# Hybrid DeltaNet and sparse attention decoder: the transposed inverse of the first doubling made by a transposition on VectorE

## The chip, the cores and the metric

The kernel runs on one core of one Trainium2 chip. The metric is the device time of one launch in microseconds (us). A core has five engines that run their own instruction queues and wait for each other by semaphores: TensorE (PE in the profile, with its weight loads as PEld), VectorE (DVE), ScalarE (ACT), GpSimd (POOL) and SyncE (SP, which issues most DMAs). TensorE's clock is granted by a throttle at one of two levels, 1.2 or 2.4 GHz; a granted clock of 1.00 is 2.4 GHz and 0.50 is 1.2 GHz.

## The reference

Two decoder layers over 528 tokens (16 meta tokens and 512). Each layer has a projection, two groups of heads side by side, an output projection, and a mixture of experts. The group that matters here is a gated DeltaNet with four heads of 128, which works in chunks and needs the inverse of a unit lower triangular matrix for every chunk and head:

```python
kb = k * beta[..., None]
lower = jnp.where(strict, jnp.einsum('bnhid,bnhjd->bnhij', kb, k) * decay, 0.0)
eye = jnp.eye(CHUNK, dtype=q.dtype)
tmat = lax.linalg.triangular_solve(eye + lower, jnp.broadcast_to(eye, lower.shape),
                                   left_side=True, lower=True, unit_diagonal=True)
u = tmat @ (v * beta[..., None])
w = tmat @ (kb * jnp.exp(gc)[..., None])
...
_, o = lax.scan(step, s0, xs)          # the recurrence over the chunks
```

Beside it, the other group of heads scores all earlier tokens with an indexer, keeps the 128 best keys of each query (`top_k`), and attends to them.

## The kernel before

**Tiling.** Tokens stand in five tiles: 16 meta tokens and four tiles of 128. The kernel uses chunks of 128 tokens where the reference has 64. Heads are handled in pairs, so one call of `invert` makes eight inverses of 128 by 128 (two heads by four tiles). There are two calls for each layer, `I0` and `I1` in the list `ORDER`, so four in a launch: they reach the changed lines at about 136 us (layer 0, pair 0), 283 us (layer 0, pair 1), 859 us (layer 1, pair 0) and 1011 us (layer 1, pair 1).

**The inversion.** `L4` is the strictly lower part, transposed. The 16 by 16 diagonal blocks are gathered through DRAM (`scr`, SP's lines 656 to 660), inverted by forward substitution on VectorE (lines 668 and 670), and brought back (`scx`, lines 673 to 680). `X` then holds the 16 by 16 inverses on the diagonal of 32 by 32 blocks, and line 683 makes `XT`, the same blocks transposed, with VectorE's transposition. Three doublings follow, from 16 to 32, 64 and 128. The first one (lines 684 to 702) makes `Y = -(L X)` masked, by 32 products of 32 by 32 (tile `y16`), then the off-diagonal blocks by products (tile `d16`), and adds them to `X` and to `XT`. Both are used below: `X` by the `y32` products and the copies to `X64`, `XT` by the copies to `F` (lines 712 and 714) and by the `d32` products. In the trace `X` and `XT` are both called `scores` (they lie in that unit's scratch), `Y` is `dn`, `F` is `lx`, and the PSUM tiles `y16` and `d16` are `y` and `d`.

**What sets the order.** The program is written in the order of `ORDER`, which mixes the work of the two groups of heads (`X` indexer, `H`, `P`, `I`, `R`, `E` DeltaNet, `S` selection, `Z`, `q`, `k`, `v` projections, `A` attention). A scheduler with its own model of durations then places the instructions of each engine, so an edit can move other instructions. Each engine runs its queue strictly in order. A product of two float32 operands through `_mm` stands as two matmuls in the trace. Projections (`project`, tile `pj`) are split into high and low parts, 24 matmuls for a half of 264 columns.

The list `ORDER`, and the helper that records all these products on line 61:

```python
ORDER = ("X0 H1 H0 P0 C0 I0 X1 H2 C1 X2 X3 C2 R0 Z0 C3 H3 q0 S1 Z1 q1 S2 P1 q2 S3 k0 q3 k1 Z3 k2 I1 k3 E0 Z2 v0 R1 v1 v2 v3 A0 S4 A1 A2 E1 A3 A4").split()
...
def _mm(nc, out, lhsT, rhs, start=True, stop=True):
    return nc.tensor.matmul(out, lhsT=lhsT, rhs=rhs, start=start, stop=stop)
```

Of the kernel before, what the change touches and what calls it, by code (L numbers as in the profile page):

```python
# [21 lines left out]
OP = mybir.AluOpType  # L22
# [37 lines left out]
def _mm(nc, out, lhsT, rhs, start=True, stop=True):  # L60
    return nc.tensor.matmul(out, lhsT=lhsT, rhs=rhs, start=start, stop=stop)  # L61
# [3 lines left out]
def trunk(ctx, tc, a, out, dbg=None, depth=DEPTH, stop=None):  # L65
    nc = tc.nc
# [207 lines left out]
    for l in range(depth):  # L274
# [93 lines left out]
        for t0, t1 in ((0, 4), (4, 5)):  # L368
            p = pc("smp")
# [50 lines left out]
        with tc.issue_after(soft.ins):  # L420
# [7 lines left out]
        p = pb("gcp")  # L428
# [10 lines left out]
                                op=OP.subtract)  # L439
# [207 lines left out]
        def invert(Hs, LT, full):  # L647
# [3 lines left out]
            X, XT = (scratch[:, 320 * i:320 * i + 320].rearrange("p (q c) -> p q c", q=10) for i in range(2))  # L651
# [15 lines left out]
            for i in range(1, 16):  # L667
                nc.vector.tensor_tensor(tv[:NB, :i, :i], Xv[:NB, :i, :i], Dv[:NB, i:i + 1, :i].to_broadcast([NB, i, i]),  # L668
                                        op=OP.mult)
# [16 lines left out]
            p = pc("y16")  # L686
            py = p[:, 0:256].rearrange("p (q c) -> p q c", q=8)
            for b in range(4):
                s = slice(32 * b, 32 * b + 32)
                for q in range(8):  # L690
                    _mm(nc, py[s, q, :], L4[s, q, s], X[s, q, :])
            Y = Db.rearrange("p (q c) -> p q c", q=8)
            nc.vector.tensor_tensor(Y, py, cst[:, None, C_M16:C_M16 + 32].to_broadcast([P, 8, 32]), op=OP.mult)
            p = pc("d16")
            pd = p.rearrange("p (x q c) -> p x q c", x=2, q=8)
            for b in range(4):
                s = slice(32 * b, 32 * b + 32)
                for q in range(8):
                    _mm(nc, pd[s, 0, q, :], XT[s, q, :], Y[s, q, :])
                    _mm(nc, pd[s, 1, q, :], Y[s, q, :], XT[s, q, :])  # L700
            nc.vector.tensor_tensor(X[:, :8, :], X[:, :8, :], pd[:, 0], op=OP.add)
            nc.vector.tensor_tensor(XT[:, :8, :], XT[:, :8, :], pd[:, 1], op=OP.add)

            F = full.rearrange("p (q i) -> p q i", q=8)
            nc.gpsimd.memset(full, 0.0)
# [3 lines left out]
            for b in range(4):  # L709
                s = slice(32 * b, 32 * b + 32)  # L710
# [6 lines left out]
            p = pc("y32")  # L717
            py = p[:, 0:256].rearrange("p (q c) -> p q c", q=8)
            Y = Db.rearrange("p (q c) -> p q c", q=8)
# [6 lines left out]
            p = pc("d32")  # L726
            pd = p.rearrange("p (x q c) -> p x q c", x=2, q=8)
# [9 lines left out]
            p = pc("y64")  # L737
            py = p.rearrange("p (q c) -> p q c", q=8)
            Y = XY
# [3 lines left out]
            p = pc("d64")  # L743
            pd = p.rearrange("p (q c) -> p q c", q=8)
# [115 lines left out]
        def delta_invert(pair):  # L860
            invert(*pairs[pair][:3])
# [155 lines left out]
        for j, src in ((0, zt), (1, so)):  # L1017
            for k in range(4):
                s = slice(k * T + q0, (k + 1) * T)
# [89 lines left out]
        for t in torder:  # L1109
            n, x = CNT[t], h[t][:CNT[t]]  # L1110
# [86 lines left out]
        for t, n in enumerate(cnts):  # L1197
            c = slice(t * 32, (t + 1) * 32)
# [32 lines left out]
        for c in range(2):  # L1231
            s = slice(64 * c, 64 * c + 64)
            nc.vector.scalar_tensor_tensor(gix[s], high[:, c, :], 8.0, low[:, c, :], op0=OP.mult, op1=OP.add)
        for c in range(2):
            s = slice(64 * c, 64 * c + 64)
# [515 lines left out]
```

## Time and profile before

| what | value |
|---|---|
| three timed runs | 1451.44, 1451.05, 1445.53 us (median 1451.05) |
| the profiled execution's own time | 1451.2 us |
| its span, first to last instruction | 1449.4 us |
| mean granted TensorE clock | 0.944 |
| TensorE busy | 1270.5 us, 88% of the span |
| VectorE, GpSimd, ScalarE busy | 788.2, 597.4, 544.1 us |

Busy shares are means over stages with different limits: in each layer, projections and the indexer come first, then selection beside the DeltaNet, then attention, then the experts. A group of rows names an engine, the line of the kernel, the operation, the tile written and the tiles read; "idle before" is the time for which the engine stood still ahead of the instruction, with what ended that. A line of stages gives, for each engine, busy time and (x) the number of its instructions in the stage, then the granted clock, the DMA engines' busy share and GB/s.

### The profile page before, as it was taken

What the parts mean: (1) busy time and instruction counts of PE and PEld (TensorE: products, weight loads), DVE (VectorE), ACT (ScalarE), POOL (GpSimd) and SP (SyncE); (2) the same over time, 40 slices, a digit from 0 to 9 for tenths busy, and PEclk for the clock granted to TensorE, in tenths of its full rate; (3) what the DMA queues carried; (4) which work ended last, traced back from release to release, by engine and by line L of the source; (5) the groups of instructions that cost most, each with busy time, mean ns of one, the idle gap of its engine ahead of it and who ended that gap; (6) DMA issues with size and microseconds to landing.
All of it is one profiled execution on the core that took longest, in us unless ns stands there. A gap on an engine that the chain in (4) does not pass through costs nothing.

```text
span 1449.4 us, 24501 instructions
## 1 busy us (share of the span) xinstructions
PE 1270.5 (88%) x8920; PEld 908.1 (63%) x8920; DVE 788.2 (54%) x2088; ACT 544.1 (38%) x1385; POOL 597.4 (41%) x779
## 2 busy tenths in 40 slices
PE   6999999899996998878588999998999789987883
PEld 6998999787883332223268988988887543322232
DVE  4887999667436141112568878995573431311116
ACT  3574544355322232223145745353453122222222
POOL 4556498845023111121255574897241231111102
PEclk9999999999997999999799999998699989999997
DMA  4252123224617999999722521222246389999991
GB/s 167 81 194 73 66 84 90 67 89 148 260 62 270 404 409 360 410 410 405 249 90 74 187 90 59 96 83 66 74 176 252 129 303 409 409 409 410 410 359 75
DMA packets 103694, 306.58 MB, mean 212 GB/s; under 512 B 24567, under 2 KB 25671, under 8 KB 103568
## 3 DMA queue, kind: packets, MB, share of 16 engines
q1 hardware_dynamic: 88464, 274.11, 49.9%
q0 software_dynamic: 9184, 18.00, 3.4%
q10 hardware_dynamic: 5920, 12.85, 2.4%
q8 instruction: 72, 1.18, 0.3%
q14 instruction: 54, 0.44, 0.1%
HBM read 281.49 MB, written 32.19 MB: 216 GB/s over the span
## 4 chain that ended last, share of the span: by engine, by line
PE 30%; DVE 7%; issue 5%; DMA 3%; ACT 3%; POOL 1%; SPq 1%; POOLq 0%; ACTq 0%; DVEq 0%; another core or an unknown queue 0%
PE pj L61 8%; PE h L61 7%; PE yp L61 4%; PE d L61 1%; PE po L987 1%; DMA ytab<-yw,dest 1%; PE lgp L61 1%; DVE dn L668 1%; PE ptp L979 1%; PE xtq L1373 1%; DVE dn L521 1%; PE y L61 1%; PE vp L61 1%; PE ix L61 1%; POOL wl L226 1%
## 5 line engine op out<-in xcount | busy, mean ns | idle before, releaser
L226 POOL TENSOR_TENSOR wl<-wr,wh 128x256 fp32r<-128x256 f32 (+1 forms) x296 | 250.3, 876 | 224.6 <-ACT wh L221 182.4
L61 PE MATMUL h<-we,xT 128*64 128x512 f32 x1024 | 229.9, 600 | 1.4 <-DMA we<-w 1.2
L61 PE MATMUL pj<-hh,wh 128*128 128x264 f32 (+2 forms) x928 | 165.3, 315 | 6.7 <-ACT raw L338 3.6
L61 PEld LDWEIGHTS h<-we,xT 128*64 128x64 f32 x1024 | 73.5, 140 | 145.5 <-issue 134.7
L61 PE MATMUL pj<-hl,wh 128*128 128x264 f32 (+2 forms) x928 | 161.8, 309 | 0.9 <-DVE rs L1624 0.9
L61 PE MATMUL pj<-hh,wl 128*128 128x264 f32 (+2 forms) x928 | 158.8, 305 | 0.0
L61 PE MATMUL yp<-we,hidT 128*64 128x512 f32 x512 | 133.2, 657 | 26.8 <-ACT yw L1355 23.1
L61 PEld LDWEIGHTS pj<-hh,wh 128*128 128x128 f32 (+1 forms) x928 | 135.1, 197 | 13.4 <-ACT raw L338 4.1
L61 PEld LDWEIGHTS pj<-hl,wh 128*128 128x128 f32 (+1 forms) x928 | 136.2, 195 | 6.8 <-DVE rs L1624 1.1
L1242 POOL MEMSET xe<- 128x1024 f32 x32 | 30.4, 952 | 263.8 <-PE h L61 249.3
L61 PEld LDWEIGHTS pj<-hh,wl 128*128 128x128 f32 (+1 forms) x928 | 131.9, 190 | 5.1 <-issue 0.4
L1325 DVE SCALAR_TENSOR_TENSOR hid<-hid,h 128x256 f32<-128x256 f32 x32 | 13.5, 421 | 212.4 <-ACT hid L1324 212.4
L221 ACT CAST wh<-wr 128x1024 fp32r<-128x1024 f32 (+1 forms) x82 | 85.5, 1046 | 92.3 <-PE pj L61 41.9
L1324 ACT ACTIVATE hid<-h 128x256 f32<-128x256 f32 x32 | 12.3, 384 | 227.3 <-PE h L61 215.9
L1380 ACT ACTIVATE xT<-xtq,lcol 128x128 f32<-128x128 f32 x192 | 73.6, 456 | 58.9 <-PE xtq L1373 58.3
L61 PEld LDWEIGHTS yp<-we,hidT 128*64 128x64 f32 x512 | 34.6, 144 | 91.7 <-issue 53.2
L1378 DVE TENSOR_SCALAR xT<-xtq,lcol 128x128 f32<-128x128 f32 x64 | 26.2, 410 | 119.3 <-ACT xT L1380 119.3
L521 DVE SCALAR_TENSOR_TENSOR dn<-cin,cw,dn 128x528 f32<-128x528 f32 x72 | 64.0, 897 | 10.8 <-ACT dn L519 9.7
L1492 POOL DMA_INDIRECT ytab<-yw,dest x28 | 28.2, 1008 | 88.4 <-ACT xT L1380 45.9
L496 DVE MATCH_REPLACE8 scores<-top,scores 128x144 f32<-128x144 f32 (+3 forms) x128 | 62.0, 487 | 0.0
L495 DVE MAX8 top<-scores 128x8 f32<-128x144 f32 (+3 forms) x128 | 60.5, 494 | 0.2
L1335 PE MATMUL hidT<-cst,hid 128*128 128x128 f32 x64 | 14.0, 300 | 39.7 <-DVE hid L1326 39.7
(432 smaller groups left out, 2488.2 us busy)
## 6 DMA issues: line engine op xcount, KB each, us to landing
we<-w SPq DMA_DIRECT2D x190, 1024.0 KB, 19.5
wr<-w_in SPq DMA_DIRECT2D x64, 512.0 KB, 3.5
wr<-w_out SPq DMA_DIRECT2D x16, 512.0 KB, 3.6
yr<-ytab SPq DMA_DIRECT2D x16, 512.0 KB, 11.8
ytab<-zr ACTq DMA_DIRECT2D x16, 264.0 KB, 3.2
hu<-x SPq DMA_DIRECT2D x8, 512.0 KB, 5.1
hs<-hu ACTq DMA_DIRECT2D x8, 512.0 KB, 4.8
ytab<-zr ACTq DMA_DIRECT2D x16, 256.0 KB, 3.2
```

What stands on the lines that cost most here:

```text
L61: return nc.tensor.matmul(out, lhsT=lhsT, rhs=rhs, start=start, stop=stop)
L221: nc.scalar.copy(hi[:, :KT * m], raw)
L226: eng.tensor_tensor(lo[:, c], raw[:, c], hi[:, c], op=OP.subtract)
L495: nc.vector.max(top, sc)
L496: nc.vector.match_replace(out=sc, in_to_replace=top, in_values=sc, imm_value=GONE)
L521: nc.vector.scalar_tensor_tensor(dst, cin[:, j:j + T], cw[:, ci + j:ci + j + 1], dst, op0=OP.mult, op1=OP.add)
L668: nc.vector.tensor_tensor(tv[:NB, :i, :i], Xv[:NB, :i, :i], Dv[:NB, i:i + 1, :i].to_broadcast([NB, i, i]), op=OP.mult)
L979: nc.tensor.transpose(p[:, (tk - 1) * P:tk * P], lg[:, OFF[tk]:OFF[tk] + P], ident)
L1242: nc.gpsimd.memset(xe, 0.0)
L1378: last = nc.vector.tensor_scalar(xT[:, kk, :], src, g_, b_, op0=OP.mult, op1=OP.add)
L1380: nc.scalar.activation(xT[:, kk, :], src, AF.Identity, bias=b_, scale=g_)
L1492: nc.gpsimd.indirect_dma_start(out=ytab[:, :], out_offset=bass.IndirectOffsetOnAxis(ap=dest[:, pair:pair + 1], axis=0), in_=yw[:, :], in_o ...
```

## The change

Before, the first doubling made two sets of products into one PSUM bank: `XT` by `Y` for `X` and `Y` by `XT` for `XT`, and VectorE added each set to its own matrix. After, only the first set is made, and `XT` is written by VectorE's 32 by 32 transposition of the updated `X`. The updated blocks are complete 32 by 32 blocks on the diagonal, so transposing each block gives the same matrix that the second set of products and its addition gave.

```diff
             p = pc("d16")
-            pd = p.rearrange("p (x q c) -> p x q c", x=2, q=8)
+            pd = p[:, 0:256].rearrange("p (q c) -> p q c", q=8)
             for b in range(4):
                 s = slice(32 * b, 32 * b + 32)
                 for q in range(8):
-                    _mm(nc, pd[s, 0, q, :], XT[s, q, :], Y[s, q, :])
-                    _mm(nc, pd[s, 1, q, :], Y[s, q, :], XT[s, q, :])
-            nc.vector.tensor_tensor(X[:, :8, :], X[:, :8, :], pd[:, 0], op=OP.add)
-            nc.vector.tensor_tensor(XT[:, :8, :], XT[:, :8, :], pd[:, 1], op=OP.add)
+                    _mm(nc, pd[s, q, :], XT[s, q, :], Y[s, q, :])
+            nc.vector.tensor_tensor(X[:, :8, :], X[:, :8, :], pd, op=OP.add)
+            nc.vector.transpose(XT[:, :8, :].rearrange("p q c -> p (q c)"), X[:, :8, :].rearrange("p q c -> p (q c)"))
```

Lines of the changed kernel behind this place have a number lower by one: the addition to `X` is line 700 there and the transposition line 701. The scheduler's order moves at some places too. Three are shown.

VectorE's queue at the first inversion (layer 0, pair 0), before: the two additions stand one behind the other (`d_1202` is the tile `d16`, `raw` a rotated projection, `lx` the matrix `F`).

```order
L348 TENSOR_TENSOR raw<-raw,ru 128x512
L483 SCALAR_TENSOR_TENSOR scores<-rel,wi,scores 128x144
L349 TENSOR_TENSOR raw<-raw,sw 128x512
L701 TENSOR_TENSOR scores<-scores,d_1202 128x256
L702 TENSOR_TENSOR scores<-scores,d_1202 128x256
L483 SCALAR_TENSOR_TENSOR scores<-ru,wi,scores 128x272
L714 COPY lx<-scores 32x8x32 x2
```

The same place in the changed kernel:

```order
L348 TENSOR_TENSOR raw<-raw,ru 128x512
L483 SCALAR_TENSOR_TENSOR scores<-rel,wi,scores 128x144
L700 TENSOR_TENSOR scores<-scores,d_1202 128x256
L349 TENSOR_TENSOR raw<-raw,sw 128x512
L701 STREAM_TRANSPOSE scores<-scores 128x256
L483 SCALAR_TENSOR_TENSOR scores<-ru,wi,scores 128x272
L713 COPY lx<-scores 32x8x32 x2
```

The addition to `X` has moved ahead of line 349, and the transposition takes the place of the second addition, behind it. At the other three inversions the transposition stands right behind the addition.

TensorE's queue at the last inversion (layer 1, pair 1), before: `y_10581` is `y16`, `d_10615` is `d16`, whose two kinds of products alternate 64 times in all, `vtp` and `vtm` are transpositions of the value projection.

```order
L61 MATMUL pj<-hl_7482,wh 128x264 x4
L61 MATMUL pj<-hh_7479,wl 128x264 x6
L61 MATMUL pj<-hh_7480,wl 128x264 x8
L61 MATMUL y_10581<-scores,lx 32x32 x32
L905 MATMUL vtp<-cst,raw 128x128 x4
L908 MATMUL vtm<-cst,raw 16x128
L61 MATMUL d_10615<-dn,scores 32x32
L61 MATMUL d_10615<-scores,dn 32x32
```

The same place in the changed kernel, on to the products of the second doubling (`y_10562`):

```order
L61 MATMUL pj<-hl_7418,wh 128x264 x4
L61 MATMUL pj<-hh_7415,wl 128x264 x8
L61 MATMUL y_10485<-scores,lx 32x32 x32
L61 MATMUL pj<-hh_7416,wl 128x264 x4
L61 MATMUL d_10519<-dn,scores 32x32 x32
L61 MATMUL pj<-hh_7416,wl 128x264 x4
L61 MATMUL y_10562<-scores,lx 32x32 x16
L904 MATMUL vtp<-cst,raw 128x128
L907 MATMUL vtm<-cst,raw 16x128
L904 MATMUL vtp<-cst,raw 128x128 x3
```

The last eight projection matmuls have moved from ahead of `y16` to behind it, in two fours, and the value's transpositions from ahead of `d16` to behind `y32`.

SP's queue ahead of the last inversion, before: `scr<-lx` and `scr<-dq` write the blocks to be inverted, `dn<-scr` brings them to VectorE, `sw<-raw` are the copies for the last key projection's rotation, `wr` are weights.

```order
L344 DMA sw<-raw 32x528
L345 DMA sw<-raw 32x528
L216 DMA wr<-w_in 128x1024
L656 DMA scr<-lx 16x8x16 x8
L659 DMA scr<-dq 16x16
L216 DMA wr<-w_in 128x1024
L660 DMA dn<-scr 66x256
```

The same place in the changed kernel:

```order
L216 DMA wr<-w_in 128x1024
L344 DMA sw<-raw 32x528
L345 DMA sw<-raw 32x528
L656 DMA scr<-lx 16x8x16 x8
L659 DMA scr<-dq 16x16
L344 DMA sw<-raw 32x528
L345 DMA sw<-raw 32x528
L660 DMA dn<-scr 66x256
```

The second half of the last key projection's copies now stands between writing the blocks and reading them back, and a weight load no longer does.

## Rows read from the trace of the kernel before

**Rows 1.** The page's part 1: engines' busy time, share of the span, instructions.

```profile
PE 1270.5 (88%) x8920; PEld 908.1 (63%) x8920; DVE 788.2 (54%) x2088; ACT 544.1 (38%) x1385; POOL 597.4 (41%) x779
```

**Rows 2.** Stages: around two inversions, the two selections behind them, the first experts.

```profile
core 0: us, PE busy (x) PEld busy (x) DVE busy (x) ACT busy (x) POOL busy (x), PEclk, DMA share, GB/s
136.00:158.50 22.50, 22.50 (x350) 21.54 (x350) 14.37 (x23) 13.48 (x29) 6.79 (x9) 1.00 0.14 49
857.00:881.00 24.00, 24.00 (x333) 23.21 (x333) 15.26 (x26) 12.73 (x27) 8.54 (x10) 0.86 0.17 60
160.00:244.00 84.00, 81.79 (x668) 78.89 (x666) 82.32 (x260) 41.09 (x132) 65.72 (x88) 1.00 0.24 76
880.00:975.00 95.00, 94.54 (x631) 84.32 (x629) 93.36 (x281) 43.61 (x120) 78.02 (x96) 1.00 0.26 85
471.00:507.00 36.00, 33.11 (x160) 11.45 (x156) 5.99 (x12) 9.03 (x22) 7.03 (x7) 1.00 1.02 404
```

**Rows 3.** The page's part 5: the experts' first matmuls, with idle time before them.

```profile
L61 PE MATMUL h<-we,xT 128*64 128x512 f32 x1024 | 229.9, 600 | 1.4 <-DMA we<-w 1.2
```

**Rows 4.** Stages, instructions of tile `d` alone: the `d16` products of the four inversions.

```profile
136.44:140.30 3.86, 3.86 (x128) 3.82 (x128) 0.00 (x0) 0.00 (x0) 1.00 0.02 4
283.34:287.20 3.86, 3.86 (x128) 3.82 (x128) 0.00 (x0) 0.00 (x0) 1.00 0.36 126
859.47:863.93 4.46, 4.46 (x128) 4.40 (x128) 0.00 (x0) 0.00 (x0) 0.83 0.01 4
1011.00:1017.40 6.40, 6.40 (x128) 6.34 (x128) 0.00 (x0) 0.00 (x0) 0.50 0.24 86
```

**Rows 5.** Stages: from `d16`'s end to `y32` in both layers; two stretches at the low clock.

```profile
140.30:143.20 2.90, 2.90 (x25) 2.76 (x23) 2.23 (x6) 2.25 (x6) 0.00 (x0) 1.00 0.00 0
863.93:869.43 5.50, 5.50 (x26) 5.36 (x24) 3.13 (x7) 3.52 (x8) 0.00 (x0) 0.52 0.27 95
862.40:869.20 6.80, 6.80 (x58) 6.73 (x52) 3.57 (x8) 3.52 (x8) 1.15 (x2) 0.50 0.21 77
1009.20:1036.50 27.30, 27.21 (x300) 22.77 (x297) 13.11 (x46) 10.28 (x32) 4.58 (x8) 0.50 0.19 68
```

**Rows 6.** VectorE in order of time (start, us): the two additions at the first inversion.

```profile
140.41 0.42 DVE L701 TENSOR_TENSOR scores<-scores,d 128x256 f32<-128x256 f32 x1 [2.70 <-PE d L61]
140.75 0.41 DVE L702 TENSOR_TENSOR scores<-scores,d 128x256 f32<-128x256 f32 x1
```

**Rows 7.** VectorE in order of time: instructions that each read the one before.

```profile
982.60 0.16 DVE L668 TENSOR_TENSOR dn<-dn 66x1 f32<-66x1 f32 x1 [1.51 <-DMA dn<-scr]
982.79 0.15 DVE L670 TENSOR_REDUCE dn<-dn 66x1 f32<-66x1 f32 x1
```

**Rows 8.** Groups by line and shape, VectorE: the transposition that exists already.

```profile
L683 DVE STREAM_TRANSPOSE scores<-scores 128x320 f32<-128x320 f32 x4 | 2.0, 509 | 0.4 <-DMA scores<-scx 0.3
```

**Rows 9.** VectorE's longest waits (total us, times, longest), 136.0 to 158.5 us.

```profile
DVE scores L701 <- PE d L61: 2.7, 1, 2.7
DVE dn L725 <- ACT dn L724: 2.2, 1, 2.2
DVE dn L521 <- ACT dn L519: 1.3, 1, 1.3
```

**Rows 10.** TensorE in order of time: the last inversion's start.

```profile
1007.70 2.12 PE L61 MATMUL y<-scores,lx 32*32 32x32 f32 x64 [1.96 <-DVE scores L681]
1009.75 1.11 PE L905 MATMUL vtp<-cst,raw 128*128 128x128 f32 x4
1010.65 0.42 PE L908 MATMUL vtm<-cst,raw 128*16 128x128 f32 x1
```

**Rows 11.** TensorE in order of time: projection matmuls at the full clock.

```profile
141.16 1.15 PE L61 MATMUL pj<-hh,wh 128*128 128x264 f32 x8
142.14 1.13 PE L61 MATMUL pj<-hl,wh 128*128 128x264 f32 x8
```

**Rows 12.** SP's queue in order of time, ahead of the last inversion.

```profile
967.91 0.59 SPq L345 DMA_DIRECT2D sw<-raw  x1
968.59 0.53 SPq L216 DMA_DIRECT2D wr<-w_in  x1
974.04 3.68 SPq L656 DMA_DIRECT2D scr<-lx  x8
```

## Prediction

> **What bounds the kernel now.** The page's first part comes first: TensorE is busy for 1270.5 of 1449.4 us, VectorE for 788.2 [rows 1]. That is a mean, so the table of stages comes next. Around the inversions TensorE stands still for nothing (22.50 of 22.50 us, 24.00 of 24.00), while VectorE idles for 8.1 and 8.7 us of the same stretches [rows 2]; the list of VectorE's waits there shows that all the long ones end by a matmul or by a ScalarE instruction that reads one [rows 9]. Behind them, in the selections, both engines are full: VectorE 82.32 of 84 us and 93.36 of 95, TensorE 81.79 and 94.54 [rows 2]. In the experts the loads run at 404 GB/s, but the first expert matmuls wait only 1.4 us in all for weights [rows 2, 3], so that stage starts when attention and routing end. The reader is to see that where the change lies TensorE's time is the path, and that an earlier TensorE must pull a full VectorE along with it to keep the gain.
>
> **The removed products.** `d16` is 128 matmuls in each inversion; the change leaves 64. They take 3.86, 3.86, 4.46 and 6.40 us [rows 4]. The four differ by the granted clock: 1.00, 1.00, 0.83 and 0.50. I cost each place by itself.
>
> *Layer 0, both pairs.* 3.86 / 2 = 1.93 us less, twice. Lower bound 0 for the first, if the selection behind it did not follow; but VectorE's 8.1 us of idle time around that place ends by TensorE or ScalarE [rows 2, 9], so its work there can start earlier by 1.9 us and the full stretch behind it, which has no such idle time, moves as a block. I take 1.9 and 1.9.
>
> *Layer 1, pair 0.* The clock fell to 1.2 GHz at 862.4 us, 2.9 us into the products, and rose again at 869.2 [rows 5]; TensorE was busy throughout. The halved set is over after about 1.9 us, so ahead of the moment at which the clock fell. In layer 0 the clock stayed at 1.00 through the whole set of 3.86 us, twice. If it stays at 1.00 here too, the stretch from the start of `d16` to `y32` becomes 1.93 + 2.90 = 4.83 us, by the like stretch in layer 0, where it was 4.46 + 5.50 = 9.96 [rows 4, 5]: 5.1 us less. If the clock falls all the same, it is 4.46 / 2 = 2.2 us. I take 5.1, since two rows of three with the whole set show no fall; VectorE's 8.7 idle us there leave room to follow.
>
> *Layer 1, pair 1.* The whole set ran at 0.50, in a stretch at that level from 1009.2 to 1036.5 us [rows 4, 5]. Half of 6.40 is 3.2 us. Against it stands a move: eight projection matmuls go from ahead of `y16` to behind it. Ahead of it they cost nothing, as TensorE waits 1.96 us there for line 681 [rows 10], which ends VectorE's and the DMAs' own chain; that wait now becomes longer. Behind it they cost 0.98 us at the full clock (the starts of two sets of eight [rows 11]) and, by 5.50 / 2.90 = 1.9 [rows 5], 1.86 us at the low one. I take the low clock, since it stood there throughout: 3.2 - 1.9 = 1.3 us less. The bounds are 1.3 and, if the clock comes back early, far more: 25 us of that stretch lie behind `y16` and would need 25 / 1.9 = 13, so up to 12 us more.
>
> **The transposition.** No row shows it on 256 columns. The nearest above is 509 ns on 320 columns [rows 8], the nearest below the addition that it replaces, 0.41 [rows 6]; I take 0.43. The second addition could start 0.34 us after the first, while the first still ran, since it did not read it [rows 6]. The transposition does read it, and such pairs start 0.03 us after the other's end [rows 7]. So `XT` is ready 0.42 + 0.03 + 0.43 = 0.88 us after the addition's start instead of 0.34 + 0.41 = 0.75, 0.13 later. At the first inversion line 349, 0.7 us, stands between them too. But the addition starts 1.9 us or more earlier, and what needs `XT` (the copies to `F`, the `d32` products) lies behind `y32`, which needs only `X`. Cost: nothing on the path. If that cover is gone it is 0.13 us each, 0.8 at the first. VectorE's busy time grows by less than 0.1 us in four.
>
> **New waits.** Behind the halved set TensorE needs `X` for `y32`, about 0.11 + 0.42 us after the last product [rows 4, 6]. At the first and third place more than 20 matmuls lie between [rows 5], at the second the order shows as many. At the last only four projection matmuls do, 0.5 us at the full clock and 0.9 at the low one: 0 to 0.2 us, inside the rounding. The scheduler's other moves in layer 1 shuffle the selection's rounds and attention's order; ahead of the last forward substitution VectorE has the same set of instructions in both orders, the transposition apart, so its full stretch keeps its length.
>
> **Sum.** 1.9 + 1.9 + 5.1 + 1.3 = 10.2 us less. The profiled execution took 1451.2 us (span 1449.4), almost the median of the timed runs, 1451.05. 1451.2 - 10.2 = 1441.0 us. About 0.5% (7.3 us) is what a measurement of this kernel can tell from no change; one of the three runs before lies 5.5 us under the others, so the forecast is not far outside it.
>
> **The rivals.**
> *VectorE swallows it.* The selections have VectorE at 98% [rows 2]. If their start is set by something other than the late matmuls, the savings of pair 0 of both layers become waits of TensorE, and only pair 1's remain: 1.9 + 1.3 = 3.2, 1448.0 us. For it: VectorE's share. Against it: what its waits ended by [rows 9].
> *The clock falls as before at layer 1, pair 0.* 1.9 + 1.9 + 2.2 + 1.3 = 7.3, 1443.9 us. The Trainium skill speaks to this, in "TensorE: Matmul & The Clock Gate", section "HAM oscillation — how this bites in real kernels": the clock drops where the engine idles between bursts while it waits for data, and every burst then starts slowly. The trace agrees at the last inversion, where a wait of 1.96 us precedes the fall [rows 10], and not at 862.4 us, where TensorE had been busy all along [rows 2]; by that rule this fall would have nothing to do with the removed products, and the time would be this rival's.
> *The products were covered, the change does nothing.* The freed time becomes TensorE waiting for `X`, since the addition and its semaphores stay: 1451 us. Against it: TensorE has 2.90 us or more of other work in between [rows 5].
> *The clock recovers in the last inversion.* With projections between its small products, as in layer 0, the 27.3 us there could shrink by up to 12 more: as low as 1429, some 1433 as a middle.
> *Slower: the low clock lasts longer.* A TensorE with fewer products between the same waits is granted 1.2 GHz for longer in the other inversions, as at the last one, for 27.3 us [rows 5]. A stretch of that length at the low clock loses 27.3 x (1 - 2.90 / 5.50) = 12.9 us. Two of them in place of the quiet ones in layer 0 give 1441.0 + 25.8 = 1466.8. It decides from 10.2 + 7.3 = 17.5 us lost, which is 37 us more at the low clock. For it: nothing in layer 0, where 3.86 us of products passed at 1.00. The other candidate for a loss, SP's queue ahead of the last inversion, has 4.9 us between the end of its last earlier issue and the writes [rows 12], so the moved copies fit.
>
> **How the numbers follow.** The forecast 0.45; the clock falls as before 0.15; VectorE swallows it 0.13; nothing 0.10; recovery 0.09; slower 0.08. Faster by over 0.5% (under 1443.8): forecast, but for 0.04 of it, recovery, and half of the clock's rival: 0.41 + 0.09 + 0.07 = 0.57. Within 0.5%: 0.04 + 0.08 + 0.13 + 0.10 = 0.35. Slower: 0.08. The range reaches from the middle of the recovery, 1433, to 1449.5, past VectorE's case; it leaves out nothing-changes, slower, and the lower part of the recovery, about 0.2. The forecast's own range is 1437 to 1444.
>
> **What would show it.** Right: `d16` with 64 matmuls in 1.9 us at the first three places and 1.9 to 3.2 at the last; the granted clock at 1.00 behind `d16` of layer 1, pair 0; the transposition near 0.43 us with TensorE not waiting for it; selection and attention starting earlier by the sums above, about 3.8 us by the end of layer 0's attention and 10 by that of layer 1. Wrong: TensorE's idle time in front of `y16`, in the selections or in the recurrence grown by as much as was saved; more stretches at 0.50 than before; `dn<-scr` of the last inversion issued late behind the key copies.

## The result, and the profile after

The changed kernel takes 1442.75 us (median of 22 runs, 1433.36 to 1450.89), the kernel before 1453.49 beside it (22 runs). The ratio is 0.9929 with a 95% interval of 0.9909 to 0.9950: faster, by 5 to 9 parts in a thousand. The profiled execution took 1439.81 us (span 1438.0), 11.4 less than that of before.

Single runs of one kernel differ by more than that, and most of it goes with the granted clock: over the 22 runs of the changed kernel, time and mean granted clock (0.935 in its slowest run, 0.946 in its fastest) correlate at -0.89. So for some kernels a second time is given, that of a straight line through the kernel's runs at one mean clock, 0.940 where nothing else is said: 1453.9 us before (29 of the 35 runs beside e1 to e4) and 1442.2 after. A run more than 1.5% above the fastest of its kernel is left out of ratios and lines. The second time has a weakness of its own: an edit can change the clock itself. A fall like that of before at layer 1, pair 0 (6.8 us at 0.50) takes 0.0023 off the mean clock of 1449 us, which by the 22 runs' 10.6 us for 0.01 is some 2.5 us (an estimate), and equal clock takes that part of a gain away.

The page's part 1 of the changed kernel, to be read against [rows 1]: TensorE has 256 instructions and 8.1 us less, VectorE as many instructions and 5.8 us more.

```profile
PE 1262.4 (88%) x8664; PEld 896.7 (62%) x8664; DVE 794.0 (55%) x2088; ACT 542.3 (38%) x1385; POOL 596.5 (41%) x779
```

Stages of the changed kernel, instructions of tile `d` alone, as in [rows 4]: 64 matmuls take 1.90, 2.02, 1.91 and 3.05 us, where 128 took 3.86, 3.86, 4.46 and 6.40.

```profile
135.90:137.85 1.95, 1.90 (x64) 1.79 (x64) 0.01 (x1) 0.00 (x0) 1.00 0.00 0
284.50:286.55 2.05, 2.02 (x64) 1.91 (x64) 0.00 (x0) 0.00 (x0) 0.92 0.23 94
857.47:859.45 1.98, 1.91 (x64) 1.79 (x64) 0.00 (x0) 0.00 (x0) 1.00 0.00 0
1001.96:1005.05 3.09, 3.05 (x64) 2.92 (x64) 0.00 (x0) 0.00 (x0) 0.50 0.00 0
```

Stages of the changed kernel, all instructions: from `d16` to `y32` at layer 1, pair 0 (the second line of [rows 5] is its like), and from line 681 of pair 0 to the first line 668 of pair 1 in either layer.

```profile
859.45:862.65 3.20, 3.20 (x25) 3.06 (x25) 2.82 (x6) 2.68 (x7) 2.42 (x3) 1.00 0.39 111
850.10:973.60 123.50, 120.69 (x999) 109.03 (x997) 119.30 (x324) 62.19 (x166) 93.89 (x119) 1.00 0.27 86
128.90:243.50 114.60, 109.85 (x1037) 106.15 (x1038) 105.84 (x293) 54.85 (x162) 77.34 (x105) 0.97 0.23 73
```

The last two stretches in the kernel before, which no row has shown yet:

```profile
852.80:982.60 129.80, 126.91 (x1075) 115.25 (x1073) 117.99 (x324) 61.75 (x162) 96.88 (x119) 0.97 0.26 82
129.40:244.10 114.70, 111.80 (x1112) 107.90 (x1112) 103.33 (x293) 54.67 (x161) 78.16 (x105) 0.99 0.23 73
```

Here lies most of the case. In layer 1 VectorE does the same 324 instructions in both kernels. It idled 129.80 - 117.99 = 11.8 us before and 123.50 - 119.30 = 4.2 after, and its busy time grew by 1.3, so the stretch is 6.3 us shorter. In layer 0 it idles 2.6 us less too (11.4 and 8.8), but its 293 instructions take 2.5 us more, and the stretch stays as it was.

VectorE in order of time at the first inversion, against [rows 6]: the transposition takes 0.44 us (0.444 is the mean of its four). No matmul waits for it; one weight load does, for 0.2 us at the last inversion.

```profile
137.84 0.42 DVE L700 TENSOR_TENSOR scores<-scores,d 128x256 f32<-128x256 f32 x1 [1.24 <-PE d L61]
138.18 0.68 DVE L349 TENSOR_TENSOR raw<-raw,sw 128x512 f32<-128x512 f32 x1
138.78 0.44 DVE L701 STREAM_TRANSPOSE scores<-scores 128x256 f32<-128x256 f32 x1
```

Two small things answer to rows ahead. The experts' first matmuls take 229.3 us and wait 0.2 ([rows 3]: 229.9 and 1.4). SP's queue ahead of the last inversion, with the moved copies, ends its last earlier issue at 962.3 and starts the writes at 964.3, so they fit ([rows 12]).

### The profile page after: what moved, and what is told of

It is laid out like the page before. It is cut to its first block, busy times and chain, and to the rows that moved or that the text cites. A ratio compares the mean times of both kernels' runs of the same rounds, so it can differ in the third digit from the quotient of the medians.

```text
span 1438.0 us, 23990 instructions
## 1 busy us (share of the span) xinstructions
PE 1262.4 (88%) x8664; PEld 896.7 (62%) x8664; DVE 794.0 (55%) x2088; ACT 542.3 (38%) x1385; POOL 596.5 (41%) x779
## 4 chain that ended last, share of the span: by engine, by line
PE 25%; DVE 12%; issue 6%; ACT 3%; DMA 2%; POOL 2%; SPq 1%; POOLq 0%; DVEq 0%; ACTq 0%; another core or an unknown queue 0%
PE h L61 7%; PE pj L61 5%; PE yp L61 4%; DVE scores L496 2%; DVE top L495 2%; PE po L986 1%; DMA ytab<-yw,dest 1%; DVE dn L668 1%; PE lgp L61 1%; PE d L61 1%; DVE dn L521 1%; PE xtq L1372 1%; PE ptp L978 1%; PE y L61 1%; POOL wl L226 1%
## 5 line engine op out<-in xcount | busy, mean ns | idle before, releaser
L61 PE MATMUL h<-we,xT 128*64 128x512 f32 x1024 | 229.3, 599 | 0.2
L61 PE MATMUL yp<-we,hidT 128*64 128x512 f32 x512 | 139.5, 684 | 26.8 <-ACT yw L1354 23.1
L1323 ACT ACTIVATE hid<-h 128x256 f32<-128x256 f32 x32 | 12.3, 383 | 229.3 <-PE h L61 217.8
L1377 DVE TENSOR_SCALAR xT<-xtq,lcol 128x128 f32<-128x128 f32 x64 | 26.2, 410 | 119.9 <-ACT xT L1379 119.9
```

The costliest lines, as they stand in the source:

```text
L1377: last = nc.vector.tensor_scalar(xT[:, kk, :], src, g_, b_, op0=OP.mult, op1=OP.add)
```

## The experiments

Durations of stages help to read them; they are differences between starts of instructions in the trace of each kernel's one profiled execution. A, C, D and F run from line 681 to line 747 (by the numbers of the kernel before), thus over one inversion each: layer 0 pair 0, layer 0 pair 1, layer 1 pair 0, layer 1 pair 1. B is the selection behind A, to the next line 668. E is what lies between D and F. One execution is not exact: with the whole set in layer 0, A is 28.7 to 33.1 and C 26.4 to 27.9 (before, e2, e3, e4).

| kernel | A | B | C | D | E | F |
|---|---|---|---|---|---|---|
| before | 28.8 | 85.9 | 26.4 | 31.1 | 123.3 | 26.0 |
| changed | 26.7 | 87.9 | 26.5 | 26.8 | 119.9 | 22.1 |
| changed, again (e10) | 27.6 | 88.3 | 26.4 | 26.7 | 119.6 | 22.2 |
| layer 0 alone (e1) | 26.7 | 87.7 | 26.5 | 30.2 | 124.2 | 24.4 |
| layer 1 alone (e2) | 33.1 | 86.0 | 27.9 | 27.5 | 119.1 | 22.1 |
| layer 1, pair 0 alone (e3) | 28.7 | 89.3 | 27.2 | 27.0 | 119.6 | 27.5 |
| layer 1, pair 1 alone (e4) | 29.6 | 86.0 | 26.3 | 32.5 | 123.5 | 26.0 |
| useless products kept (e5) | 29.6 | 87.0 | 30.9 | 32.5 | 123.5 | 25.7 |
| four useless products (e6) | 29.0 | 88.6 | 26.6 | 27.3 | 120.5 | 21.3 |
| turned loops (e7) | 25.4 | 85.9 | 22.9 | 26.1 | 119.3 | 18.3 |
| before, turned loops (e8) | 24.9 | 86.1 | 22.9 | 26.6 | 124.3 | 18.3 |

### One place at a time

Four kernels make the products and additions of before except where a condition holds:

```diff
+            turned = l == 0          # e2: l == 1; e3, e4: one pair of layer 1
             for b in range(4):
...
                     _mm(nc, pd[s, 0, q, :], XT[s, q, :], Y[s, q, :])
-                    _mm(nc, pd[s, 1, q, :], Y[s, q, :], XT[s, q, :])
+                    if not turned:
+                        _mm(nc, pd[s, 1, q, :], Y[s, q, :], XT[s, q, :])
```

> The changed form in layer 0 alone; layer 1 keeps the 128 products and the two additions. By the forecast's terms 1.9 + 1.9 = 3.8 us less than the kernel before (ratio 0.9974), all of it in place when layer 0's attention ends. By the trace of the changed kernel layer 0 brings only about 2 us (0.9986), because VectorE's full stretch behind the first inversion gives some of the 2.6 us back, and at the second inversion TensorE gains under 1 us. If the whole gain belongs to layer 1's order, 0.

Measured: 1450.59 us, ratio 0.998 (0.9949 to 1.0011); at clock 0.940 1450.5, 3.4 under before. The interval holds 3.8 us and 0. The trace sides with the second number: A is 2.1 us shorter, B 1.8 longer, C unchanged.

A is longest in e2, 33.1, which has layer 0 as before: there the clock fell within the whole set of pair 0, at 139.5 us for 6.8, and in e5 within that of pair 1 (C 30.9). So the fall that before shows at layer 1 alone comes in layer 0 too, in two of ten inversions with the whole set (before, e2 to e5), and in or right behind none of eight with half of it (changed twice, e1, e6). From line 681 of the first inversion to the router of layer 0, which follows attention, the executions take 307.5 to 312.6 us with the whole set (before, e2, e3, e4) and 306.3 to 311.2 with half. The forecast 3.8 can't be told from that spread.

> The changed form in layer 1 alone. By the forecast's terms 5.1 + 1.3 = 6.4 us less than the kernel before (0.9956), with the clock at 1.00 behind the first set. By the trace of the changed kernel about 9 us (0.994): 4.5 at the first inversion, the rest ahead of and in the last one. If layer 0 and layer 1 are independent, this ratio and that of the layer 0 kernel multiply to that of the whole change, 0.993.

Measured: 1450.47 us, 0.9975 (0.9940 to 1.0009); at clock 0.940 1447.8, 6.1 under before. By the trace D, E and F gain 3.6, 4.2 and 3.9. The timed runs lie nearer the forecast's 6.4 than that sum of 11.7, which neither reading reaches; the same execution is 4.4 and 1.4 longer in A and C, where nothing was changed. The ratios of e1 and e2 multiply to 0.9955, the whole change has 0.9929; with intervals of 0.003 on each the two don't differ.

> The changed form at layer 1, pair 0 alone; the scheduler's order ahead of the last inversion is already that of the changed kernel, with the eight projection matmuls behind y16, while the last inversion keeps its 128 products. By the forecast's terms 5.1 us less, and a loss of up to 1.9 from the moved projections: 3.2 to 5.1 (0.9965 to 0.9978). If the new order itself brings part of the gain, 6 to 7 us (0.9955), seen as line 681 of the last inversion earlier by clearly more than line 747 of the first. If the clock falls at this place in spite of the halved set, 2.2 us.

Measured: 1444.22 us, 0.9954 (0.9925 to 0.9982); at clock 0.940 1449.9, 4.0 under before. The clock did not fall behind `d16`, E is as short as in the changed kernel although the last inversion keeps its 128 products, and F, with eight projection matmuls moved behind `y16` at the low clock and nothing saved, is 1.5 longer. So part of the gain lies in E, behind the halved products, and comes with the new order.

> The changed form at layer 1, pair 1 alone; the scheduler keeps the order of the kernel before there, with all 32 projection matmuls ahead of y16. By the forecast's terms the products bring 3.2 us without the loss of 1.9, if the clock stays low through the set (0.9978); with the clock back at 1.00 in the set 1.9 or less (0.9987). If the gain of the last inversion came from the new order and not from the products, 0: line 747 would then move by less than 1 us against line 681.

Measured: 1454.09 us, 1.0001 (0.9963 to 1.0039); at clock 0.940 1451.5, 2.4 under before. `d16` there takes 3.06 us instead of 6.40, yet F is 26.0 as before. TensorE in order of time around it:

```profile
1007.71 1.11 PE L910 MATMUL vtp<-cst,raw 128*128 128x128 f32 x4
1008.61 0.42 PE L913 MATMUL vtm<-cst,raw 128*16 128x128 f32 x1
1008.97 3.06 PE L61 MATMUL d<-dn,scores 32*32 32x32 f32 x64
1011.95 1.13 PE L61 MATMUL lgp<-sk,qs 128*128 128x144 f32 x4
```

`y32` starts 3.4 us sooner behind line 681 than before (7.9 against 11.3). Between there and line 747 the scheduler put 3.4 us more of attention's matmuls (`lgp`, `ptp`, `po`): 18.1 against 14.7. The saving is real and was spent on the spot, on work that is then done earlier.

### Are the products the gain?

The transposition makes `XT`, and the 64 products that made it before are issued all the same, into a half of the PSUM tile that nobody reads:

```diff
                     _mm(nc, pd[s, q, :], XT[s, q, :], Y[s, q, :])
+                    _mm(nc, pw[s, 1, q, :], Y[s, q, :], XT[s, q, :])
```

> XT is made by the transposition, but the 64 matmuls per inversion that made it before are still issued, into a half of the PSUM tile that nobody reads; the scheduler leaves the order nearly as in the kernel before. If the gain is TensorE's time in these matmuls, all of it is gone: ratio to the kernel before 0.998 to 1.002, d16 with 128 matmuls near 3.9 us, and the clock falls at layer 1, pair 0 behind them as in three kernels with the whole set. If the transposition itself, off TensorE, were what helps (a shorter VectorE chain, one PSUM read less), the time would be that of the changed kernel, 0.993.

Measured: 1460.43 us, 1.0023 (0.9985 to 1.0061). All of the gain is gone, and stages D, E and F are near those of before (D 1.4 longer). Its runs had a low clock, 0.936 in the mean; at 0.940 it takes 1452.5 us and the runs of before beside it 1455.5, 3.0 apart where the change makes 11.7. So the transposition by itself brings nothing that these runs can tell. Products and order are not parted here: e5 puts the products back, and with them the order is nearly that of before. Stages at layer 1, pair 0, `d16` and what follows it:

```profile
873.10:877.10 4.00, 4.00 (x121) 3.99 (x121) 1.00 (x2) 0.85 (x2) 2.97 (x4) 0.85 0.01 4
877.10:882.00 4.90, 4.90 (x31) 4.83 (x29) 2.48 (x6) 3.25 (x8) 0.00 (x0) 0.50 0.35 107
```

The third column from the end is the granted clock. It falls here, as in e1 (0.62 behind `d16`), e4 (0.52) and before (0.52 [rows 5]): four kernels of four with the whole set of 3.86 us. It stays at 1.00 in the changed kernel twice, in e2, e3 and e6: five executions of five with half the set in this sequence. From `y16` on TensorE was busy in both kinds, but for at most 0.3 us. (In e11, below, whose order is another, it falls ahead of `d16`, at 853.0 us, for 6.8.)

### The order by itself

The changed kernel, with four useless products at layer 1, pair 0 (`8 * b + q < 4` in place of all 32), was to have its products in the order of before.

> The changed kernel with four useless products (eight matmuls of 0.03 us) added at layer 1, pair 0 alone. They cost 0.24 us, but with them the scheduler gives layer 1 the order of the kernel before: 32 projection matmuls ahead of the last y16, and VectorE's selection rounds and the L600 products as before. If the products alone are the gain, the time stays that of the changed kernel, 0.993. If the order brings 3 to 4 of layer 1's 9 us, the stretch from line 747 of the first inversion to the first line 668 of the last is about 99 us and not 96.5, with a wait of 1.5 to 1.9 us for the blocks' way through DRAM, and the ratio is 0.995 to 0.996. The clock should still not fall behind d16 of layer 1, pair 0.

Measured: 1445.12 us, 0.9926 (0.9888 to 0.9964). The premise failed: its trace shows a third order, neither of the two (28 projection matmuls ahead of the last `y16`, four behind it, most of the value's last projection between `d16` and `y32`), and line 600 early as in the changed kernel. It says only that another order around the halved products does as well. No kernel here has half the set with the order of before, so the order by itself stays untested.

What E owes to the order is read from the traces instead. VectorE's longest wait in E, kernel e4:

```profile
DVE dn L668 <- DMA dn<-scr: 1.9, 1, 1.9
```

and the changed kernel at the same place, in order of time, to be read against [rows 7]:

```profile
972.85 0.85 DVE L637 TENSOR_SCALAR dk<-vtq,nk 128x128 f32<-128x128 f32 x3
973.63 0.14 DVE L668 TENSOR_TENSOR dn<-dn 66x1 f32<-66x1 f32 x1
```

Line 600 makes the blocks, which go through DRAM to line 668. In before, e1, e4 and e5 VectorE has 18 instructions between the two and then waits 1.5, 2.4, 1.9 and 1.8 us. In every kernel with half the set at layer 1, pair 0, e12 apart (13, and 0.7), it has 21 to 24 there, and waits 0.0. The scheduler moved line 600 forward, and the way through DRAM is covered. That this makes E short is argued and not shown: e11 waits 0.0 too, and its E is 123.6; e8, with the whole set and turned loops, has 22 instructions, waits 1.0, and its E is 124.3.

### The same products in another sequence

In `y16` and `d16` eight products in a row lie on one 32 by 32 block of TensorE's array. The loops are turned round in the changed kernel:

```diff
-            for b in range(4):
-                s = slice(32 * b, 32 * b + 32)
-                for q in range(8):
+            for q in range(8):
+                for b in range(4):
+                    s = slice(32 * b, 32 * b + 32)
                     _mm(nc, pd[s, q, :], XT[s, q, :], Y[s, q, :])
```

> The changed kernel with the loops of y16 and d16 turned round, so that matmuls that follow each other lie on different 32 by 32 blocks of the array; the order around them stays that of the changed kernel but for small moves. The d32 set, which lies like that already, starts a matmul every 21.5 ns by its records, y16 and d16 every 30 ns. If the block is the reason, y16 and d16 take about 1.4 us instead of 1.9 each, 1 us per inversion and twice that at the low clock: 3 to 5 us in all, ratio to the kernel before near 0.990. If d32 is quick for another reason, y16 and d16 stay at 1.9 us and the ratio at 0.993.

Measured: 1431.15 us (6 runs), 0.9827 (0.9774 to 0.9881). The direction was right, the size more than twice as large as expected (3 to 5 us under the changed kernel). TensorE in order of time, layer 1, pair 0 of that kernel:

```profile
850.99 0.77 PE L61 MATMUL y<-scores,lx 32*32 32x32 f32 x64 [0.85 <-DVE scores L681]
...
855.95 0.75 PE L61 MATMUL d<-dn,scores 32*32 32x32 f32 x64
...
859.90 1.09 PE L61 MATMUL y<-scores,lx 32*32 32x32 f32 x32
```

64 matmuls take 0.75 us instead of 1.91, 11.7 ns each instead of 30; even at the low clock of the last inversion 1.08 instead of 3.06. `y32`, whose loops were left, keeps 1.09 for 32. The Trainium skill, "TensorE: Matmul & The Clock Gate", section "Part 3: Packing small matmuls — row/col tiling", says that matmuls on different blocks of the array run side by side, and that a weight load overlaps a running matmul only where the rows differ. These rows agree with both and don't part them: with the block, the partitions read and written change too.

> The kernel before, with both sets of d16 products and both additions, and the loops of y16 and d16 turned round so that four matmuls in a row lie on the four different diagonal blocks of the array. In the run before this one 64 such matmuls took 0.75 us instead of 1.91. If that holds here, d16's 128 take about 1.5 us instead of 3.86 and y16 0.75 instead of 1.93, 3.5 us per inversion at the full clock, and the kernel before needs the transposition hardly any more: ratio 0.984 to 0.987, within 0.5% of the turned loops with the transposition. If the two sets disturb each other (each product of the second set loads what the first one streamed), d16 stays above 2.5 us and the ratio at 0.99 or above.

Measured: 1431.56 us (6 runs), 0.9849 (0.9791 to 0.9907). The whole set at layer 1, pair 0, tile `d` alone:

```profile
858.70:860.30 1.60, 1.29 (x128) 1.18 (x128) 0.00 (x0) 0.00 (x0) 1.00 0.00 0
```

128 matmuls take 1.29 us, less than 64 did. With the loops turned, the change of this case takes 1.29 - 0.75 = 0.5 us of products away per inversion, and the medians of e8 and e7 lie 0.4 apart. That does not make the rest of the change worthless. The six runs of e8 had the better clock, 0.949 in the mean against 0.944. At 0.945, which the runs of all these kernels enclose, half the products (e10) lie 10.4 us under the runs of before beside them, turned loops (e8) 9.2 and both (e7) 20.1, each to within some 3 us: there the two nearly add. In the two traces attention of layer 1 ends 8.6 us later without the transposition (1140.6 against 1132.0), 5.0 of it in E; its experts then took 231.8 us against 238.2. That much the experts differ between executions of other kernels too (231.3 in e1, 238.2 before, with the same layer 1), but whether e8's better clock over six runs is a trait of the kernel these runs don't tell, and so it stays open how much of the change is left once the loops are turned: 0.4 us by the medians, 9 at equal clock.

> The changed kernel with the loops of y16, d16 and y32 turned round; y32's 32 matmuls then alternate between two blocks. If two blocks in turn go twice as fast, y32 falls from 1.09 to about 0.6 us, 0.5 us per inversion, 2 us in all at most: ratio to the kernel before 0.981 to 0.983. If VectorE's and ScalarE's reads of y32, which no longer find their half done early, take it back, 0.983, as with the two loops alone.

Measured: 1430.23 us (6 runs), 0.9827 (0.9782 to 0.9872): `y32` falls from 1.09 to 0.69 us, and the time does not move against e7.

> The changed kernel once more, on the same chip and beside the same runs of the kernel before as the two kernels with turned loops: 0.991 to 0.995 by its own earlier interval; the turned loops are then compared with it directly.

Measured: 1441.19 us, 0.992 (0.9884 to 0.9955), on the chip of e8 and e9. e9, the fastest kernel of the study, is 11 us under it there (8 at clock 0.945).

### Where layer 0's gain went

In both kernels line 575 is a product of 128x5. GpSimd in order of time, kernel before:

```profile
224.78 1.33 POOL L348 TENSOR_TENSOR qT<-raw,ru 128x528 f32<-128x528 f32 x1
226.06 1.33 POOL L349 TENSOR_TENSOR raw<-raw,sw 128x528 f32<-128x528 f32 x1
```

VectorE at the same time, kernel before:

```profile
224.76 1.37 DVE L575 TENSOR_TENSOR nk<-nk,rk 128x5 f32<-128x5 f32 x1
226.05 0.56 DVE L495 MAX8 top<-scores 128x8 f32<-128x400 f32 x1
```

GpSimd in the changed kernel:

```profile
222.45 1.33 POOL L348 TENSOR_TENSOR qT<-raw,ru 128x528 f32<-128x528 f32 x1
223.74 1.32 POOL L349 TENSOR_TENSOR raw<-raw,sw 128x528 f32<-128x528 f32 x1
```

VectorE in the changed kernel:

```profile
222.43 2.65 DVE L575 TENSOR_TENSOR nk<-nk,rk 128x5 f32<-128x5 f32 x1
225.00 0.56 DVE L495 MAX8 top<-scores 128x8 f32<-128x400 f32 x1
...
226.16 1.88 DVE L592 TENSOR_TENSOR dq<-dq,dn 128x512 f32<-128x512 f32 x1
```

Before, the little product ends 0.02 us after GpSimd's first instruction; after, it misses that gap and ends 0.02 us after the second one. Over twelve executions it is always one or the other: 1.37 us in before, e2, e4, e5, e7 and e8, whose B is 85.9 to 87.0, and 2.64 to 2.68 in the changed kernel twice, e1, e3, e6 and e9, whose B is 87.7 to 89.3. e3 has layer 0 as before, so the halved products need not come first for it. The Trainium skill, "SBUF — State Buffer", section "Who interferes with whom", has the rule: a VectorE instruction with two inputs in SBUF and a GpSimd instruction that reads SBUF share a port, and the later one is blocked. The rows agree that VectorE's instruction lasts until GpSimd's ends. Which of the two was the later one they don't show: line 575 starts within 0.02 us of line 348, mostly ahead of it, while GpSimd's instruction before that, line 226, still had some 0.05 us to run.

```diff
-            nc.vector.tensor_tensor(nk, nk, rk, op=OP.mult)
+            nc.gpsimd.tensor_tensor(nk, nk, rk, op=OP.mult)
```

> The changed kernel with one 128x5 product, line 575, moved from VectorE to GpSimd in all eight heads; the scheduler's order moves at many places with it. In layer 0 that instruction, with two SBUF inputs, took 2.65 us on VectorE in every kernel whose stretch from line 747 of the first inversion to the first line 668 of the second was 87.7 us or more, and 1.37 in those at 85.9 to 87.0, each time to the end of a GpSimd product. If VectorE's wait for GpSimd is what gives layer 0's gain back, no VectorE product of 128x5 there takes over 2 us and the stretch is 86 us or less, unless another product with two SBUF inputs falls into the same gap; the time then is 2 to 4 us under the changed kernel's, ratio 0.990. If the late selection has another reason, the stretch stays near 88 us.

Measured: B is 85.2 us, as expected, and line 681 of the second inversion comes at 271.0 instead of 275.6. The whole kernel took 1451.93 us, 0.9979 (0.9943 to 1.0016): the time expectation missed. The scheduler's new order lost more in layer 1: the way from line 668 to line 681 of pair 0 takes 29.0 us instead of 24.0, E 123.6, F 26.6. With so much moved, B alone is not a clean proof either.

> The kernel with the turned loops of y16 and d16, and with all four 128x5 products of a head (lines 571 to 575) on GpSimd. VectorE is full in the selections, and these 32 products take it some 18 us in all by their groups of rows, 1 to 2.6 us each where they wait for GpSimd. If that time comes off VectorE's full stretches, up to 10 us less than with the turned loops alone, ratio to the kernel before 0.976; if GpSimd, with its own longer instructions and the order that the scheduler then makes, takes it back, 0.983 or above.

Measured: 1434.86 us (6 runs), 0.9852 (0.9809 to 0.9896), no better than e7. VectorE was relieved, by 6.8 us in all (793.4 to 786.6 busy; the four lines had taken 14.9 in e7, not some 18), but B grew to 95.0 and E to 124.8. In B the new order gives VectorE 12 instructions and 7.3 us more than in e7. From line 681 of layer 1's pair 0 to the next line 668 it is the idle time that grew, from 3.5 to 9.3.

## Why the prediction was right, and where its terms were not

The time was right, 1441.0 forecast and 1442.75 measured, and so was the main mechanism: with the removed products put back (e5) the gain is gone, and the largest term, the clock at layer 1, pair 0, held. But three terms were mis-sized, and that they cancelled is luck.

**Layer 0, 1.9 + 1.9.** In the trace it gave 2.1 + 0 by line 747, and 2.0 of that went again in B. The step that failed is "the full stretch behind it ... moves as a block". It starts earlier by 2.6 us, but it is not stiff: its instructions grew by 2.5 us mainly because those of two lines met GpSimd's: line 592 takes 2.3 us more in B, line 575 1.3 more (and line 499 1.3 less). That it gave the gain back is the rival "VectorE swallows it" in the outcome, though not by its reason. At pair 1 the loss is the clock. TensorE's wait ahead of `y16` grew from 3.4 to 4.1 us, the low clock came at 274.6 for 10.2 us instead of at 278.7 for 3.4, and the way from `y16` to `d16` took 8.4 us instead of 6.4. That eats the 1.9 saved. It is the same in e1, e6 and e10 (10.2 us each; 3.4 to 6.8 in before and e2 to e5), and the slower rival's mechanism, at under a tenth of its price. The rule that the prediction cites from the Trainium skill, "TensorE: Matmul & The Clock Gate", section "HAM oscillation — how this bites in real kernels", agrees here: the clock falls at 274.6, inside the wait that ends at 276.1. By the timed runs of e1 layer 0 is worth 3.4 us at equal clock, so its net value stays between that and nothing.

**Layer 1, pair 0, 5.1.** From `d16`'s start to `y32` it took 5.18 us (857.47 to 862.65) instead of 9.96: 4.8 less, and 4.3 by line 747. The step "the clock doesn't fall" held in five executions of five, against the rival in which the clock falls as before.

**Left out of the sum: 3.4 us in E.** "VectorE has the same set of instructions in both orders ... so its full stretch keeps its length" was wrong in its second half. The set is the same, but four of its instructions moved behind line 600, the wait of 1.5 us that [rows 7] showed is gone, and VectorE's wait for the blocks' way back, at line 681, fell from 7.4 us to 4.9. That the order causes this is argued, as said above.

**Layer 1, pair 1, 1.3.** F is 3.9 shorter, and 1.2 comes back between line 747 and the router (117.6 to 118.8 us). TensorE in order of time, changed kernel, against [rows 10]:

```profile
997.79 3.06 PE L61 MATMUL y<-scores,lx 32*32 32x32 f32 x64 [5.28 <-DVE scores L681]
1000.78 1.25 PE L61 MATMUL pj<-hh,wl 128*128 128x264 f32 x4
1001.96 3.06 PE L61 MATMUL d<-dn,scores 32*32 32x32 f32 x64
1004.94 1.25 PE L61 MATMUL pj<-hh,wl 128*128 128x264 f32 x4
1006.12 1.73 PE L61 MATMUL y<-scores,lx 32*32 32x32 f32 x32
```

The wait grew from 1.96 to 5.28 as foreseen, the products saved 3.3 (forecast 3.2), the projections cost 2.4 (1.9), and `y16`, now wholly at the low clock, 0.9, which the sum had not. What it had not either is that the value's transpositions and four `lgp` matmuls, 2.3 us together, no longer stand ahead of `y32`. From `y16` to `y32` that makes 8.3 us instead of 10.8. Another 2.0 of F's 3.9 lie between `y32` and line 747, where 15 of attention's matmuls stand instead of 25; they come later, as the 1.2 shows.

**The transposition** costs 0.44 us (0.43 forecast), and no matmul waits for it. **More stretches at the low clock** did not come: 160 us of the span against 164.

By the router of layer 1 the changed kernel is 13.1 us ahead (forecast 10), 2.7 of it from ahead of layer 1's first inversion, and the experts, where the stretches at the low clock lie elsewhere in every execution, take 1.7 back. These are sums over one execution: in e10, the same kernel again, it is 7.7 ahead at the router and gains 5 in the experts.

## What to carry to other kernels

Before taking products away from TensorE, look at their sequence: where small products in a row lie on the same block of the array, turning a loop can bring as much as halving their number. Compare kernels at equal clock as well as by their medians before saying what one leaves for the other. A saved microsecond is kept only by the stage that has no slack of its own; follow it from line to line through the engine that is full, by that engine's busy time and idle time apart, to see where it stays. And where the scheduler orders the work, its answer to an edit may weigh as much as the edit.

## What the runs showed that was not expected

- Products of 32 by 32 on one block take 30 ns a matmul (the set's time by its count), on four blocks in turn 11.7 ns at the full clock and 17 at the low one; 128 of two kinds, four of each in turn over the four blocks, take 10 ns each.
- A VectorE product of 128x5 with two inputs in SBUF takes 0.15 us alone, and up to 1.37 or 2.65 beside GpSimd's products, to the end of the first or second of them.
- From run to run of one kernel, 0.01 of mean granted clock goes with 10.6 us (22 runs of the changed kernel), as much as the whole change.
